# A gate projection: the input's forms at another byte, a second pass that takes two groups by sums, and a combination made in its result tiles

## The chip, the cores and the metric

The kernel runs on one core of one Trainium2 chip. The metric is the device time of one execution in microseconds (us). Three executions of the kernel before took 1046.55, 1047.09 and 1047.61 us: a median of 1047.09 us.

TensorE (PE) multiplies; VectorE (DVE), ScalarE (ACT) and GpSimd (POOL) do everything else; SyncE (SP) issues the loads of the weights. Each engine takes its instructions in the order in which the program lists them for it.

## The reference

One layer of a gated linear attention mixer and a squared-ReLU MLP, on 256 tokens of width 2048, all in float32. Cut to what matters:

```python
def layer(x):                                    # x: 256 x 2048
    h = rmsnorm(x, gla_norm)
    q, k, v, r, g_low = split(h @ w_in)          # w_in: 2048 x 6160; r: 256 x 2048
    log_a = log_sigmoid(g_low @ w_gate_up + b_gate) / 16
    o = chunked_gated_scan(q, k, v, log_a)       # 4 heads, chunks of 64 tokens
    o = o * rsqrt(mean(o * o) + eps) * o_norm    # per head of 512 columns
    x = x + (o * silu(r)) @ w_out
    a = relu(rmsnorm(x, mlp_norm) @ w_up)        # 256 x 8192
    x = x + (a * a) @ w_down
    return rmsnorm(x, final_norm)
```

The change concerns the product that gives `r`, and what is done with it.

## The kernel before, in words

**High and low parts.** TensorE multiplies in a float32 form of reduced precision. So each operand is kept as a high part (a copy in that form) and a low part (the value less its high part), and a product is three matmuls: high by high, high by low, low by high (`multiply`, L664 to L670; the matmul itself is L669). The weights arrive as plain float32. ScalarE makes the high part of each piece (L1201), VectorE the low part (L1207). A matmul here always has a stationary block of 128 x 128 and 256 moving columns.

**Gate projection.** `r` is made in four passes c = 0 to 3 of 512 columns. Each pass has four groups g of four K tiles of 128 rows, so a group's weights are 128 partitions x 2048 elements, 1 MB. A group of a pass is called a double, (c,g). It is done in one of two ways:
- plain (`plain_double`): the tokens are stationary, the weights move, 48 matmuls;
- by sums (`sums_double`): a 2 x 2 block scheme that needs seven products of blocks where the plain way needs eight. 24 matmuls read parts of the weights as they are, and 18 read sums of blocks of them, 42 in all. On the token side the scheme needs sums of the input too. These are the input's forms `x_forms` (L536), made once for g = 2 and 3, and kept in a tile named `h` in the trace.

What a sums double needs of the weights is made as follows. First the block add: a quarter of the weights is added to another, in place. In this projection VectorE does it (first line of `adds`, L859); in the later product with `w_out` ("o") GpSimd issues a DMA within SBUF that accumulates (`add_block`, L845). Then VectorE makes three sums of blocks (rest of `adds`), ScalarE their high part (L869 and L870), and VectorE their low part (L520). The sums have one buffer (`sums`), and so have their parts (`sumshl`), so that two sums doubles can't be prepared far apart from their use. The weights have three buffers (`rawu0` to `rawu2`) and three of high and low parts (`high`, `low`), taken in turn.

**Banks and the combination.** A pass by sums accumulates in four banks of PSUM: T0B, T1B, B16 and B50. A plain pass takes two, T0B and T1B. Banks come from one list: who needs a bank takes the first, who is done appends it. After a pass by sums, `combine_parts` (L945) puts the four banks together: ScalarE copies B16 to SBUF (L949), VectorE does six additions and subtractions (L519 and L520, four of 128 x 256 and two of 128 x 512). The scratch for that is `ends`, the first half of the tile `sums` (L581). Then each half goes through a silu on ScalarE (L982) and is multiplied into the attention's result `on` on VectorE (L986). After a plain pass `gated` (L921) does the silu out of the bank.

**Attention in between.** Between the parts of pass 0 stand the eight products of the attention ("attends", four heads of two token tiles). Each puts its result in a bank. ScalarE squares it and sums up (`attend_square`, L892), VectorE scales the sum (L898), GpSimd takes its power of -1/2 (`rsqrt`, L314) and multiplies it by a factor of the token (L902). Last ScalarE puts the scaled result into `on` (`attend_put`, L906), and only then is the bank free.

**The order.** The doubles before, in program order: pass 0 plain 0, sums 2, plain 1, sums 3, with an attend at each gap; pass 1 plain 0, 1, 2, 3; pass 2 plain 0, sums 2, eight transposes, plain 1, sums 3; pass 3 plain 0 to 3. A plan sets the order of all other work: `at(time, run)` enters it with a time counted in matmuls of TensorE's program, all entries are sorted by it, and each engine gets its instructions in that order. `chunk` enters the high and low parts and the load of a group (L842, on SyncE's queue). For a plain double of a later pass of the gate projection these stand 89, 70 and 173 ahead of its first matmul; for a sums double 80, 63 and 204, the three adds 94, the casts of the sums 50 and 41, the low part of the sums 30. `place_chunks` assigns the three places for parts in order of the high parts.

**The result of a pass.** `some512` gives a tile of 128 x 512, named `sr` in the trace, one for each half of the tokens.

Of the kernel before, what the change touches and what calls it, by code (L numbers as in the profile page):

```python
# [70 lines left out]
def tile_gla_mlp(ctx, tc, x, xt, w_vg, w_in, w_gate, w_out, w_up, w_down, final_norm, out):  # L71
# [460 lines left out]
    def sums_of_rows(a):  # L532
        return a.rearrange("p (n b f s) -> p n b f s", n=2, b=2, f=4)

    hbuf = h_tile(F32R)
    x_forms = {g: sums_of_rows(hbuf[:, OFF + n * 2 * G : OFF + (n + 1) * 2 * G]) for n, g in enumerate((2, 3))}  # L536
    on = None

    def take_on():
# [38 lines left out]
    slot += [a_slot(1), a_slot(2)]  # L578
    by_form = lambda a: a.rearrange("p (f b c) -> p f b c", f=3, b=2)
    sums = by_form(flat_sums)  # L580
    ends = flat_sums[:, : 3 * T].rearrange("p (f s) -> p f s", f=3)  # L581
    sums_to = o_stage = None

    def take_sums():
# [33 lines left out]
    def at(time, run):  # L618
        plan.append((time, len(plan), run))
# [151 lines left out]
    plain_double("r", 0, 1, between=one_attend)  # L771
    sums_double("r", 0, 3, between=one_attend)
    end_of("r", 0)
    for g in range(4):
        plain_double("r", 1, g)
    end_of("r", 1)
    plain_double("r", 2, 0)
    sums_double("r", 2, 2)
# [54 lines left out]
    for n, (p, c, g, summed_) in enumerate(doubles):  # L833
# [10 lines left out]
        def add_block(view=view):  # L844
            nc.gpsimd.dma_start(out=view[:, :, 1, left], in_=view[:, :, 1, right], accum_op=ALU.add)  # L845

        here = p == "r"
        if not summed_:
            early = 14 if here and c else 0
            chunk(key, time - UP_HI - early, time - UP_LO - early, time + 2 * UP, (time - UP_EARLY - 3 * early, load), raw)  # L850
            continue
        early = 13 if here and c else 0
        chunk(key, time - 67 - early, time - 50 - early, time + RAWS, (time - 165 - early, load), raw)
        if not here:
            at(time - 116, add_block)

        def adds(view=view, here=here):
            if here:
# [6 lines left out]
            sub(sums_to[1], sums, sums_to[0].bitcast(F32))  # L865
            done.add(("sums", key))

        at(time - 68 - 2 * early, adds)
        at(time - 50, lambda: nc.scalar.copy(sums_to[0][:, :2], sums[:, :2]))  # L869
        at(time - 41, lambda: nc.scalar.copy(sums_to[0][:, 2], sums[:, 2]))  # L870
        at(time - 30, low)
# [61 lines left out]

        return run, times

    for c in (1, 3):
        e = mark("end", "r", c)
        for t in range(NT):
            run, times = gated(c, t, None)
            at(e - 5 + 6 * t, run)  # L940
            at(e + 2 + 7 * t, times)

    pair = lambda a: a.rearrange("p (i s) -> p i s", i=2)

    def combine_parts(p, c, out0, out1):  # L945
        pc = p, c

        def first():
            nc.scalar.copy(ends[:, 1:3].rearrange("p f s -> p (f s)"), bank_of[pc, B16])  # L949
            release(pc, B16)  # L950

        def second():
            sub(ends[:, 2], ends[:, 1], ends[:, 2])
            sub(ends[:, 0], bank_of[pc, B50][:, left], ends[:, 2])
            add(pair(out0()), pair(bank_of[pc, T0B]), ends[:, 0:2])
            release(pc, T0B)

        def third():
            both = bank_of[pc, B50][:, right]
            add(ends[:, 0], both, ends[:, 0])  # L960
            sub(ends[:, 2], ends[:, 2], both)
            release(pc, B50)
            add(pair(out1()), pair(bank_of[pc, T1B]), ends[:, 0::2])
            release(pc, T1B)

        e = mark("end", p, c)
        for n, run in ((-11, first), (-6, second), (1, third)):
            at(e + n, run)
        return e

    for c in (0, 2):
        zs = {}

        def new(t, zs=zs):
            zs[t] = some512()
            return zs[t]

        e = combine_parts("r", c, lambda new=new: new(0), lambda new=new: new(1))
        for t in range(NT):

            def silu(t=t, zs=zs):
                nc.scalar.activation(zs[t], zs[t], AF.Silu, scale=r1[:, t : t + 1])  # L982

            def times(c=c, t=t, zs=zs):
                o = on[:, t, c * GT : (c + 1) * GT]
                nc.vector.tensor_tensor(o, o, zs[t], op=ALU.mult)  # L986

            at(e + 4 + 8 * t, silu)
            at(e + 11 + 8 * t, times)
# [618 lines left out]
```

## Time and profile before

| what | value |
|---|---|
| median of three executions | 1047.09 us (1046.55 to 1047.61) |
| profiled execution: its time | 1046.55 us |
| its span | 1044.7 us |
| mean granted clock of TensorE | 0.998 |
| busy: PE, DVE, ACT, POOL | 1036.4, 850.8, 689.7, 92.5 us |
| chain of waits: share of PE | 98% |
| DMA | 228.21 MB, mean 218 GB/s |

The trace is of one execution. Its time is 1.85 us more than its span, which begins at the first and ends at the last recorded instruction. Times in rows are microseconds from the span's start. A row of a timeline has the start, the duration, the engine, the line, the operation and tiles (written <- read), the shape, the types, how many equal ones follow each other, and, in square brackets, the idle time of the engine just before it with what ended it. A tile's number is left out there. A row of a table of windows has the window, its length, then for PE, weight load, DVE, ACT, POOL and SyncE the busy time and the count, then the granted clock, the busy share of the DMA engines, and GB/s. The gate projection runs from about 150 to 325 us.

### The profile page before, as it was taken

What the parts mean: (1) busy time and instruction counts of PE and PEld (TensorE: products, weight loads), DVE (VectorE), ACT (ScalarE), POOL (GpSimd) and SP (SyncE); (2) the same over time, 40 slices, a digit from 0 to 9 for tenths busy, and PEclk for the clock granted to TensorE, in tenths of its full rate; (3) what the DMA queues carried; (4) which work ended last, traced back from release to release, by engine and by line L of the source; (5) the groups of instructions that cost most, each with busy time, mean ns of one, the idle gap of its engine ahead of it and who ended that gap; (6) DMA issues with size and microseconds to landing.
All of it is one profiled execution on the core that took longest, in us unless ns stands there. A gap on an engine that the chain in (4) does not pass through costs nothing.

```text
span 1044.7 us, 21232 instructions
## 1 busy us (share of the span) xinstructions
PE 1036.4 (99%) x9050; PEld 1036.2 (99%) x9050; DVE 850.8 (81%) x856; ACT 689.7 (66%) x824; POOL 92.5 (9%) x105
## 2 busy tenths in 40 slices
PE   9999999999999999999999999999999999999997
PEld 9999999999999999999999999999999999999997
DVE  7568657667687776899989989989989999999894
ACT  7675545574575664667677677777767667768763
POOL 0000000120000001010101101011111101010000
PEclk9999999999999999999999999999999999999999
DMA  9857664454766576787878778787788788787652
GB/s 346 310 164 212 194 201 147 137 199 164 263 191 215 155 267 193 217 256 226 231 228 250 223 223 252 222 234 231 223 246 236 211 255 232 208 255 229 201 208 81
DMA packets 117438, 228.21 MB, mean 218 GB/s; under 512 B 6192, under 2 KB 22576, under 8 KB 117216
## 3 DMA queue, kind: packets, MB, share of 16 engines
q1 hardware_dynamic: 99920, 208.84, 60.5%
q0 software_dynamic: 16320, 15.73, 9.7%
q10 hardware_dynamic: 1104, 2.29, 0.6%
q8 instruction: 70, 1.15, 0.4%
q14 instruction: 24, 0.20, 0.0%
HBM read 209.02 MB, written 2.10 MB: 202 GB/s over the span
## 4 chain that ended last, share of the span: by engine, by line
PE 98%; issue 1%; ACT 0%; DVE 0%; POOLq 0%; POOL 0%; ACTq 0%
PE acc L1363 21%; PE acc L1243 18%; PE aux L1243 16%; PE acc L669 12%; PE acc L149 11%; PE acc L181 6%; PE aux L669 4%; PE aux L1363 4%; PE aux L181 2%; PE aux L149 2%; PE aux L216 0%; PE acc L739 0%; PE acc L479 0%; PE aux L479 0%; ACT sqf L1497 0%
## 5 line engine op out<-in xcount | busy, mean ns | idle before, releaser
L1207 DVE TENSOR_TENSOR low<-rawu,high 128x2048 fp32r<-128x2048 f32 (+1 forms) x101 | 224.6, 2226 | 26.3 <-ACT high L1201 24.3
L1201 ACT CAST high<-rawu 128x2048 fp32r<-128x2048 f32 (+1 forms) x101 | 187.4, 1857 | 47.2 <-DMA rawu<-in_w_up 12.6
L1243 PE MATMUL acc<-hh,high 128*128 128x256 f32 x544 | 150.6, 277 | 0.0
L1243 PE MATMUL acc<-hh,low 128*128 128x256 f32 x544 | 150.5, 277 | 0.0
L1243 PE MATMUL acc<-hl,high 128*128 128x256 f32 x544 | 150.5, 277 | 0.0
L1412 ACT CAST sumshl<-sums 128x1024 fp32r<-128x1024 f32 x112 | 88.2, 835 | 94.0 <-PE acc L1363 70.6
L1207 DVE TENSOR_TENSOR low<-rawd,high 128x2048 fp32r<-128x2048 f32 (+1 forms) x59 | 132.8, 2252 | 17.7 <-ACT high L1201 17.7
L1201 ACT CAST high<-rawd 128x2048 fp32r<-128x2048 f32 (+1 forms) x59 | 111.4, 1890 | 44.8 <-PE acc L1243 36.7
L520 DVE TENSOR_TENSOR sumshl<-sums,sumshl 128x1536 fp32r<-128x1536 f32 x64 | 112.3, 1755 | 25.2 <-ACT sumshl L1412 24.7
L1243 PE MATMUL aux<-hh,high 128*128 128x256 f32 x480 | 132.8, 277 | 0.0
L1243 PE MATMUL aux<-hl,high 128*128 128x256 f32 x480 | 132.8, 277 | 0.0
L1243 PE MATMUL aux<-hh,low 128*128 128x256 f32 x480 | 132.7, 277 | 0.0
L1363 PE MATMUL acc<-high,acts 128*128 128x256 f32 x598 | 116.0, 276 | 0.0
L119 DVE TENSOR_TENSOR lo<-raw,hi 128x1024 fp32r<-128x1024 f32 (+3 forms) x68 | 78.7, 1164 | 44.3 <-ACT hi L118 44.1
L1399 POOL DMA_DIRECT2D rawd<-rawd x56 | 67.6, 1207 | 515.4 <-DVE sums L519 264.5
L118 ACT CAST hi<-raw 128x1024 fp32r<-128x1024 f32 (+3 forms) x68 | 67.7, 1001 | 56.0 <-PE acc L181 25.7
L1243 PEld LDWEIGHTS acc<-hh,high 128*128 128x128 f32 x544 | 102.2, 188 | 0.0
L1243 PEld LDWEIGHTS acc<-hl,high 128*128 128x128 f32 x544 | 102.2, 188 | 0.0
L1243 PEld LDWEIGHTS acc<-hh,low 128*128 128x128 f32 x544 | 102.2, 188 | 0.0
L1363 PEld LDWEIGHTS acc<-high,acts 128*128 128x128 f32 x598 | 96.6, 188 | 0.0
L1363 PE MATMUL acc<-sumshl,acts 128*128 128x256 f32 x720 | 96.0, 276 | 0.0
L1243 PEld LDWEIGHTS aux<-hh,high 128*128 128x128 f32 x480 | 90.2, 188 | 0.0
(346 smaller groups left out, 2788.1 us busy)
## 6 DMA issues: line engine op xcount, KB each, us to landing
rawu<-in_w_up SPq DMA_DIRECT2D x124, 512.0 KB, 4.5
rawd<-in_w_down SPq DMA_DIRECT2D x56, 1024.0 KB, 5.1
raw<-in_w_in SPq DMA_DIRECT2D x48, 512.0 KB, 4.7
rawu<-in_w_in SPq DMA_DIRECT2D x16, 1024.0 KB, 5.0
rawu<-in_w_out SPq DMA_DIRECT2D x16, 1024.0 KB, 5.8
rawd<-rawd POOLq DMA_DIRECT2D x56, 256.0 KB, 5.3
rawu<-in_w_down SPq DMA_DIRECT2D x16, 512.0 KB, 4.4
raw<-in_w_vg SPq DMA_DIRECT2D x13, 520.0 KB, 8.4
```

Source lines behind the costliest of these rows:

```text
L118: last_hi[0] = nc.scalar.copy(hi[:, s], raw[:, s])
L119: last_lo[0] = nc.vector.tensor_tensor(lo[:, s], raw[:, s], hi[:, s].bitcast(F32), op=ALU.subtract)
L149: nc.tensor.matmul(o[:, m], x, w[:, m], start=first and c == 0, stop=last, skip_group_check=True)
L181: nc.tensor.matmul(o, u[:, s], m[:, kt], start=kt == 0 and n == 0 and j % 2 == 0, stop=kt == KT - 1 and n == 2, skip_group_check=True,)
L520: sub = lambda o, x, y: nc.vector.tensor_tensor(o, x, y, op=ALU.subtract)
L669: nc.tensor.matmul(b[:, o], a[x], w[y], start=(pc, name) in fresh, stop=last and i == 2, skip_group_check=True)
L1201: nc.scalar.copy(o, i)
L1207: nc.vector.tensor_tensor(o, i, x.bitcast(F32), op=ALU.subtract)
L1243: nc.tensor.matmul(o, w[:, s], row_h(kt)[m], start=kt == 0 and n == 0 and j % 2 == 0, stop=kt == KT - 1 and n == 2, skip_group_check=True,)
L1363: nc.tensor.matmul(bank[:, o], a[x], w[y], start=fresh and i == 0, stop=d + 1 in starts + [SUMMED] and i == 2, skip_group_check=True,)
L1399: nc.gpsimd.dma_start(out=view[:, :, 1, left], in_=view[:, :, 1, right], accum_op=ALU.add)
L1412: nc.scalar.copy(sums_to[0][:, f], sums[:, f])
```

## The change

Three things are edited.

1. The input's forms lie at the start of their tile, where they stood 48 elements (192 bytes) behind it. Counted in SBUF, their blocks then start at byte 192 modulo 256, where they started at byte 128.
2. Pass 1 is done as plain 0, sums 2, plain 1, sums 3, where it was plain 0 to 3. Its two block adds are done by the accumulating DMA on GpSimd's queue, not by VectorE; passes 0 and 2 keep VectorE's.
3. `combine_parts` has no scratch of its own: ScalarE copies the bank B16 in two halves into the two result tiles, and the four small and two large operations work in place there. It is used for passes 0, 1 and 2 of `r` and for passes 1 and 3 of `o`; pass 1's silu thus comes from the result tile and no longer from the bank.

```diff
     hbuf = h_tile(F32R)
-    x_forms = {g: sums_of_rows(hbuf[:, OFF + n * 2 * G : OFF + (n + 1) * 2 * G]) for n, g in enumerate((2, 3))}
+    x_forms = {g: sums_of_rows(hbuf[:, n * 2 * G : (n + 1) * 2 * G]) for n, g in enumerate((2, 3))}
...
-    ends = flat_sums[:, : 3 * T].rearrange("p (f s) -> p f s", f=3)
...
-    for g in range(4):
-        plain_double("r", 1, g)
+    plain_double("r", 1, 0)
+    sums_double("r", 1, 2)
+    plain_double("r", 1, 1)
+    sums_double("r", 1, 3)
     end_of("r", 1)
...
-        here = p == "r"
+        here = p == "r" and c != 1
         if not summed_:
-            early = 14 if here and c else 0
+            early = 14 if p == "r" and c else 0
...
-        early = 13 if here and c else 0
+        early = 13 if p == "r" and c else 0
         chunk(key, time - 67 - early, time - 50 - early, time + RAWS, (time - 165 - early, load), raw)
         if not here:
-            at(time - 116, add_block)
+            at(time - 116 - early, add_block)
...
-        at(time - 68 - 2 * early, adds)
+        at(time - 68 - (2 if here else 0) * early, adds)
...
-    for c in (1, 3):
+    for c in (3,):
...
-    pair = lambda a: a.rearrange("p (i s) -> p i s", i=2)
-
     def combine_parts(p, c, out0, out1):
         pc = p, c
+        z = []
 
         def first():
-            nc.scalar.copy(ends[:, 1:3].rearrange("p f s -> p (f s)"), bank_of[pc, B16])
+            z.extend((out0(), out1()))
+            for i, o in enumerate((left, right)):
+                nc.scalar.copy(z[i][:, right], bank_of[pc, B16][:, o])
             release(pc, B16)
 
         def second():
-            sub(ends[:, 2], ends[:, 1], ends[:, 2])
-            sub(ends[:, 0], bank_of[pc, B50][:, left], ends[:, 2])
-            add(pair(out0()), pair(bank_of[pc, T0B]), ends[:, 0:2])
-            release(pc, T0B)
+            sub(z[1][:, right], z[0][:, right], z[1][:, right])
+            sub(z[0][:, left], bank_of[pc, B50][:, left], z[1][:, right])
 
         def third():
             both = bank_of[pc, B50][:, right]
-            add(ends[:, 0], both, ends[:, 0])
-            sub(ends[:, 2], ends[:, 2], both)
+            add(z[1][:, left], both, z[0][:, left])
+            sub(z[1][:, right], z[1][:, right], both)
             release(pc, B50)
-            add(pair(out1()), pair(bank_of[pc, T1B]), ends[:, 0::2])
-            release(pc, T1B)
+            for i, name in enumerate((T0B, T1B)):
+                add(z[i], bank_of[pc, name], z[i])
+                release(pc, name)
...
-    for c in (0, 2):
+    for c in range(3):
```

From the second edit on, line numbers of the changed kernel are one lower (lines 581 to 772) to two higher than those of the kernel before.

The order of the instructions moves with it. In the rows below, numbers behind a name tell buffers of one name apart, and the square brackets name what is waited for: the other engines, DMAHW for loads, DMASW for DMAs of GpSimd's queue.

GpSimd, before, from the factor of the second head (`ors_2558`) to that of the fourth (`ors_2731`):

```order
L902 TENSOR_TENSOR ors_2558<-ors_2558,r1k_127 128x2 [waits Pool_49]
L314 TENSOR_TENSOR ors_2643<-oss_2583,mhalf_116 128x1 [waits DVE_49]
L314 TENSOR_TENSOR ors_2643<-oss_2583,mhalf_116 128x1 [waits Activation_49]
L902 TENSOR_TENSOR ors_2643<-ors_2643,r1k_127 128x2 [waits Pool_49]
L314 TENSOR_TENSOR ors_2731<-oss_2672,mhalf_116 128x1 [waits DVE_49,Activation_49]
L314 TENSOR_TENSOR ors_2731<-oss_2672,mhalf_116 128x1 [waits Activation_49]
```

And now; `rawu2` holds the weights of (1,2), `rawu1` those of (1,3):

```order
L903 TENSOR_TENSOR ors_2558<-ors_2558,r1k_127 128x2 [waits Pool_49]
L846 DMA rawu2_2348<-rawu2_2348 128x2x256 [waits DMAHW4_49,DMAHW5_49,DMAHW3_49,DMAHW6_49,DMAHW2_49,DMAHW7_49,DMAHW1_49,DMAHW0_49]
L314 TENSOR_TENSOR ors_2644<-oss_2583,mhalf_116 128x1 [waits DVE_49]
L314 TENSOR_TENSOR ors_2644<-oss_2583,mhalf_116 128x1 [waits Activation_49]
L903 TENSOR_TENSOR ors_2644<-ors_2644,r1k_127 128x2 [waits Pool_49]
L846 DMA rawu1_2347<-rawu1_2347 128x2x256 [waits DMAHW6_49,DMAHW1_49]
L314 TENSOR_TENSOR ors_2740<-oss_2674,mhalf_116 128x1 [waits DVE_49,Activation_49]
```

The two block adds stand between the factors of the heads, the first one behind that of the second head and the second one behind that of the third.

ScalarE around the same place, before: `rawu2` holds the weights of (1,1), `aux_1893` and `aux_1894` are the two banks of the third head's attends, `acc_1763` is pass 0's B16.

```order
L892 ACTIVATE sq_2640,oss_2583<-aux_1894,r1k_127 128x512 [waits PE_49,Activation_49]
L1201 CAST high2_2351<-rawu2_2348 128x2048 [waits DMAHW7_49]
L892 ACTIVATE sq_2673,oss_2672<-acc_1765,r1k_127 128x512 [waits PE_49,Activation_49]
L906 ACTIVATE on_1999<-aux_1893,ors_2643 128x512 [waits Pool_49]
L949 COPY sums_2345<-acc_1763 128x512 [waits DVE_49,PE_49]
L906 ACTIVATE on_1999<-aux_1894,ors_2643 128x512
L892 ACTIVATE sq_2708,oss_2672<-acc_1766,r1k_127 128x512 [waits PE_49,Activation_49]
L982 ACT_TABLE_LOAD
L982 ACTIVATE sr_2694<-sr_2694,r1_126 128x512 [waits DVE_49]
```

And now, with `rawu2` those of (1,2):

```order
L893 ACTIVATE sq_2641,oss_2583<-aux_1894,r1k_127 128x512 [waits PE_49,Activation_49]
L1202 CAST high2_2351<-rawu2_2348 128x2048 [waits DMAHW7_49,DMASW0_49]
L893 ACTIVATE sq_2675,oss_2674<-acc_1765,r1k_127 128x512 [waits PE_49,Activation_49]
L907 ACTIVATE on_1999<-aux_1893,ors_2644 128x512 [waits Pool_49]
L951 COPY sr_2694<-acc_1763 128x256 [waits PE_49,Activation_49]
L951 COPY sr_2695<-acc_1763 128x256 [waits Activation_49]
L907 ACTIVATE on_1999<-aux_1894,ors_2644 128x512
L870 CAST sumshl_2357<-sums_2345 128x1024 [waits DVE_49,PE_49]
L893 ACTIVATE sq_2714,oss_2674<-acc_1766,r1k_127 128x512 [waits PE_49,Activation_49]
L1202 CAST high0_2343<-rawu0_2346 128x2048 [waits DMAHW0_49]
L983 ACT_TABLE_LOAD [waits DVE_49]
L983 ACTIVATE sr_2694<-sr_2694,r1_126 128x512 [waits Activation_49]
```

The high part now also waits for the block add (DMASW), and behind it stands the put of `aux_1893`, the bank that the first matmul of (1,0) takes. A cast of sums and a high part stand ahead of the first silu that were not there before.

VectorE, before, from the low part of (1,0) (`low1_2350`) to the combination of pass 0 (`sr_2694` and `sr_2712` are its result tiles):

```order
L1207 TENSOR_TENSOR low1_2350<-rawu1_2347,high1_2349 128x2048 [waits DMAHW6_49,Activation_49]
L898 TENSOR_SCALAR oss_2583<-oss_2583 128x2 [waits Activation_49]
L1207 TENSOR_TENSOR low2_2352<-rawu2_2348,high2_2351 128x2048 [waits DMAHW7_49,PE_49,Activation_49]
L520 TENSOR_TENSOR sums_2345<-sums_2345 128x256 [waits Activation_49]
L520 TENSOR_TENSOR sums_2345<-acc_1764,sums_2345 128x256 [waits DVE_49,PE_49]
L519 TENSOR_TENSOR sr_2694<-acc_1895,sums_2345 128x512 [waits DVE_49]
```

And now:

```order
L1208 TENSOR_TENSOR low1_2350<-rawu1_2347,high1_2349 128x2048 [waits DMAHW6_49,Activation_49]
L899 TENSOR_SCALAR oss_2583<-oss_2583 128x2 [waits Activation_49]
L519 TENSOR_TENSOR sums_2345<-rawu2_2348 128x512 [waits DMAHW7_49,DMASW0_49,DVE_49]
L519 TENSOR_TENSOR sums_2345<-sums_2345,rawu2_2348 128x512 [waits DVE_49]
L520 TENSOR_TENSOR sums_2345<-sums_2345,rawu2_2348 128x512
L1208 TENSOR_TENSOR low2_2352<-rawu2_2348,high2_2351 128x2048 [waits PE_49,Activation_49]
L520 TENSOR_TENSOR sr_2695<-sr_2694,sr_2695 128x256 [waits Activation_49]
L520 TENSOR_TENSOR sr_2694<-acc_1764,sr_2695 128x256 [waits DVE_49,PE_49]
L519 TENSOR_TENSOR sr_2695<-acc_1764,sr_2694 128x256 [waits DVE_49]
L520 TENSOR_TENSOR sr_2695<-sr_2695,acc_1764 128x256
L519 TENSOR_TENSOR sr_2694<-acc_1895,sr_2694 128x512 [waits DVE_49]
```

Three adds stand between the scale of the third head and the low part, the first of them waiting for the block add; and both large operations of the combination now stand last.

## The prediction

> **What bounds the kernel now.** I read the page first, then TensorE's waits, then its pace stage by stage, and last VectorE's margins in the gate projection (pass c and group g of it: "(c,g)"; pass 1 is the "second gate pass").
>
> ```profile
> PE 1036.4 (99%) x9050; PEld 1036.2 (99%) x9050; DVE 850.8 (81%) x856; ACT 689.7 (66%) x824; POOL 92.5 (9%) x105
> PE aux L216 <- DVE square L213: 1.1, 1, 1.1
> 161.00:198.00 37.00, 37.00 (x329) 37.00 (x328) 25.23 (x30) 19.67 (x22) 0.00 (x0) 1.00 0.43 143
> 199.00:252.00 53.00, 53.00 (x452) 53.00 (x451) 38.55 (x40) 33.63 (x42) 10.36 (x12) 1.00 0.57 189
> 262.00:293.00 31.00, 31.00 (x266) 31.00 (x265) 20.52 (x22) 17.53 (x19) 0.00 (x0) 1.00 0.71 241
> L669 PE MATMUL acc<-high,h x24: 274/281/283, 198.5 to 263.1; 128*128 128x256 f32 x24
> ```
>
> TensorE never waits after its first microsecond, so time is matmuls times pace. The three stretches (length, then matmuls in brackets) give 37.00/329 = 112.5 ns, 53.00/452 = 117.3 and 31.00/266 = 116.5 ns at a full clock. The pace falls by about 4.4 ns as the first stationary block from `h` (the input's forms) comes at 198.5, and the matmuls on other operands between them are slow too.
>
> The second thing to see is how little VectorE is ahead here:
>
> ```profile
> 244.75 1.75 DVE L520 TENSOR_TENSOR sumshl<-sums,sumshl 128x1536 fp32r<-128x1536 f32 x1
> 250.90 0.88 PE L669 MATMUL acc<-sumshl,h 128*128 128x256 f32 x6
> 274.21 2.29 DVE L1207 TENSOR_TENSOR low<-rawu,high 128x2048 fp32r<-128x2048 f32 x1
> 276.73 0.28 PE L669 MATMUL acc<-low,xh 128*128 128x256 f32 x1
> 219.00:253.00 34.00, 34.00 (x291) 34.00 (x290) 26.55 (x28) 20.16 (x21) 1.26 (x3) 1.00 0.55 185
> ```
>
> The low part of (2,2)'s sums ends at 246.50 and is used at 250.90: 4.4 us early. The low part of (3,2) ends at 276.50 and is used at 276.73: 0.2 us early. Between these two ends VectorE's line takes 30.0 us, waits included. In 219 to 253 it is busy 26.55 of 34.00 us.
>
> **What the change gives.** Two plain doubles of 48 matmuls become sums doubles of 42: 12 x 0.1125 = 1.35 us. The forms move by 192 bytes to where the other stationary blocks lie. If that keeps the pace, some 735 matmuls between 198.5 and 293 (the 452 and 266 of the slow stretches, and their edges) gain 4.4 ns each, 3.25 us. With nothing late that is 4.6 us. The rows show the pace beside the tile, not its cause; for the 3.25 I take all, the other end is 0.
>
> The Trainium skill speaks against this term: "TensorE: Matmul & The Clock Gate", section "Back-to-back issue gap", gives a gap set by the number of columns alone, whatever the place of the operands. By it the two stretches would have one pace; the rows 4.4 ns apart at one clock disagree, and by it the sum would be 1.35 us instead of 4.6.
>
> **What it adds.** VectorE gets, in pass 1, twice three adds and a low part of sums, six operations of a combination, and no block add. The rows for these:
>
> ```profile
> 308.50 0.69 DVE L519 TENSOR_TENSOR sums<-rawu 128x512 f32<-128x512 f32 x1
> 310.49 2.29 DVE L1207 TENSOR_TENSOR low<-rawu,high 128x2048 fp32r<-128x2048 f32 x1
> 312.70 1.75 DVE L520 TENSOR_TENSOR sumshl<-sums,sumshl 128x1536 fp32r<-128x1536 f32 x1
> 314.37 2.29 DVE L1207 TENSOR_TENSOR low<-rawu,high 128x2048 fp32r<-128x2048 f32 x1
> ...
> 219.67 0.42 DVE L520 TENSOR_TENSOR sums<-sums 128x256 f32<-128x256 f32 x1
> 222.90 0.69 DVE L986 TENSOR_TENSOR on<-on,sr 128x512 f32<-128x512 f32 x1
> 223.51 0.16 DVE L898 TENSOR_SCALAR oss<-oss 128x2 f32<-128x2 f32 x1
> 235.78 0.68 DVE L519 TENSOR_TENSOR rawu<-rawu 128x512 f32<-128x512 f32 x1
> 237.84 0.68 DVE L520 TENSOR_TENSOR sums<-sums,rawu 128x512 f32<-128x512 f32 x1
> ```
>
> Start to start: three adds 1.99, a low part 2.21, a low part of sums 1.67, a combination 3.23, a product with `on` 0.61, four adds 2.7. Pass 1 adds 2 x 3.66 + 3.23 = 10.5 us: 26.55 + 10.5 = 37 us of VectorE in a stretch that TensorE would pass in 34.0 - 1.35 - 1.3 = 31.4. The 4.4 us of lead don't cover 5.7.
>
> Worse is where the block add of (1,2) goes. GpSimd's queue takes it behind the second head's factor; ScalarE's high part and VectorE's first add then wait for its landing, each with its queue behind it.
>
> ```profile
> 207.63 4.19 POOL L314 TENSOR_TENSOR ors<-oss,mhalf 128x1 f32<-128x1 f32 x2 [4.05 <-DVE oss L898]
> 211.90 1.78 POOL L902 TENSOR_TENSOR ors<-ors,r1k 128x2 f32<-128x2 f32 x1
> 213.65 0.37 SPq L842 DMA_DIRECT2D rawu<-in_w_in  x1
> 300.73 1.35 POOL L845 DMA_DIRECT2D rawu<-rawu  x1 [75.58 <-issue]
> 300.98 0.37 SPq L842 DMA_DIRECT2D rawu<-in_w_out  x1
> 312.81 0.37 SPq L842 DMA_DIRECT2D rawu<-in_w_out  x1
> 313.19 1.21 POOL L845 DMA_DIRECT2D rawu<-rawu  x1 [11.11 <-DVE low L1207]
> 320.41 0.69 DVE L519 TENSOR_TENSOR sums<-rawu 128x512 f32<-128x512 f32 x1 [3.76 <-issue]
> DMA to landing us min/median/max: 3.6/5.5/7.7
> ```
>
> The factor ends at 211.90 + 1.78 = 213.68; with TensorE 0.3 us earlier by then, the add is issued at 213.4. The four block adds of this form took 3.6 to 7.7 us to land (last row). The two with a weight load issued within 0.4 us (300.98 beside 300.73, 312.81 beside 313.19) are the long ones: the second held VectorE until 320.41, 7.2 us. SyncE's row at 213.65 is the load that will be (1,3)'s, as before (only (1,2)'s and (1,1)'s change places): it waits for the low part of (1,0), at whose end GpSimd's factor ends too, so it starts beside the new add. So I take 7.4, of the 3.6 to 7.7 that bound it: **landing at 220.8**, where VectorE's queue would reach the adds at about 216.
>
> ScalarE: behind the high part stand a square, then the put that frees the bank for (1,0)'s first matmul.
>
> ```profile
> 194.45 1.04 ACT L869 CAST sumshl<-sums 128x1024 fp32r<-128x1024 f32 x1
> 215.53 1.91 ACT L1201 CAST high<-rawu 128x2048 fp32r<-128x2048 f32 x1
> 217.32 0.70 ACT L892 ACTIVATE sq<-acc,r1k 128x512 f32<-128x512 f32 x1
> 217.99 0.70 ACT L906 ACTIVATE on<-aux,ors 128x512 f32<-128x512 f32 x1
> 219.03 0.73 ACT L906 ACTIVATE on<-aux,ors 128x512 f32<-128x512 f32 x1
> 219.79 0.28 PE L669 MATMUL aux<-high,xh 128*128 128x256 f32 x1
> 220.85 1.28 ACT L982 ACT_TABLE_LOAD   x1
> ```
>
> From 215.53 to the end of the put, 218.69, is 3.2 us; so (1,0) starts at 220.8 + 3.2 = 224.0, where it stood at 219.79: 4.2 us late at once. (Pass 1 now takes four banks for two; the third and fourth are first written by (1,2), 5.4 us after (1,0)'s start, and free by then: the combination of pass 0 reads the last of them at about 227.) The high part, square, put, copy and second put (to 219.76, 4.2 us), a cast of sums (0.95), a square (0.67), a high part (1.8), the table load (1.28, no longer ahead of the wait) and a silu (0.7) put the first silu's end 9.6 us behind the landing; VectorE, with three adds, a low part and a combination (7.4), waits 2.2 us for it.
>
> VectorE from the landing to the end of (2,2)'s low part of sums: five low parts 11.05, three low parts of sums 5.0, adds 6.7, two combinations 6.45, three products 1.85, a copy 0.35: 31.4 us, and waits for ScalarE of 2.2, 0.3 and 0 to 1 (0.5): 34.4 us. That is 255.2 against 246.50. TensorE alone, from 224.0 over 252 matmuls, would be there at 252.4: VectorE binds. From there the 30.0 us of line to (3,2) are unchanged in work (its first silu comes 1.2 us later, since both adds stand last; the shorter copies give part of it back), while TensorE, from 250.90 to 276.73, needs 25.8, and 25 at the better pace. (3,2) starts at 285.3 for 276.73: 8.5 us late. The rest of the stage, some 147 matmuls, gains 0.65 back. Nothing later changes but the copy of the combination, 0.5 us on ScalarE, under matmuls at a margin of 3 us.
>
> Sum: 1046.55 (the profiled execution) + 8.5 - 0.65 = 1054.4; it lay 0.54 below the median, so **1054.9**.
>
> **Rivals.**
> 1. The add lands alone, 3.6 to 3.9 us after 213.4, because the load of (1,3) is served behind it. For it: the two short adds; against it: the loads 0.25 and 0.38 us from the long ones. All of the sum is 3.7 us earlier: 1051.2.
> 2. The wait cools TensorE. The last matmuls and the clock after them (the eighth figure of the windows):
>
> ```profile
> 1036.64 0.84 PE L149 MATMUL acc<-hl,acts 128*128 128x256 f32 x6
> 1040.00:1044.70 4.70, 0.00 (x0) 0.00 (x0) 0.00 (x0) 0.02 (x1) 0.00 (x0) 0.53 0.58 225
> 1.06 4.63 PE aux L216 x20
> ```
>
> The clock is near half from about 3 us after the last matmul; at the start 4.6 us passed before full pace. The wait at (1,0), about 5 us, is that long; those from (3,0) to (3,2) come to 5 us in pieces. At (1,0) the loss vanishes under VectorE, which is 2.8 us later than TensorE at (2,2); at (3,2) half a rate over 4.6 us costs up to 2.3: 1057.2. The Trainium skill has this as a rule ("TensorE: Matmul & The Clock Gate", section "Part 1: The HAM clock gate"): a free-running window of about 3.4 us without work drops the clock to half. By that rule a wait of 4 or 5 us may or may not hold a whole window.
> 3. Faster: VectorE keeps up. The 30.0 us of its line hold 6.8 us of waits (row below); if they vanish as TensorE comes earlier, and the add has landed by 213, when VectorE reaches it, nothing is late and all 4.6 us stay: 1042.5.
>
> ```profile
> 246.50:276.50 30.00, 23.19 (x28) 1.00 0.59 198
> ```
>
> For it: some of these waits are for TensorE, and come earlier with it. Against it: GpSimd is held to 213.7 by its factor. The point from which it decides: with the waits as they are, a landing at 213.0, 7.8 us before mine, gives the time of before. With half of this, an early landing and half the waits gone, the time is about 1047.
> 4. The place of the forms does nothing to the pace: the sum loses only the last 0.65, as VectorE binds anyway: 1055.5.
>
> **How the numbers follow.** Forecast 0.55, with its own range 1052.8 to 1056.8 (landing 219 to 222, the waits 0 to 1); rival 1 0.18; rival 2 0.10; rival 4 0.05; rival 3 0.05, its half 0.07. The range 1049.3 to 1057.5 leaves out rival 3 with its half and the far ends of 1 and 2. A measurement of this kernel tells about 0.2%, 2.1 us, from no change: faster 0.05 (rival 3), same 0.08 (its half, and the near edge of rival 1), slower 0.87.
>
> **What would show it.** Right: a wait of TensorE of 3 to 6 us ahead of (1,0), put down to ScalarE; some 5 us in all ahead of (3,0) to (3,2) for VectorE, most at (3,2); a block add from about 213.5 that lands near 220.8; a pace of 112.5 ns from 199 to 252 outside the waits; 9038 matmuls. Wrong: no idle time of TensorE in 219 to 286, or a landing before 214; then the sum of VectorE's line is what failed. A pace of 117 ns there takes the 3.25 away.

## The result, and the profile after

Five executions of the changed kernel took 1055.97 to 1059.32 us, with a median of 1057.6 us; the kernel before took 1047.09 us beside them. The ratio is 1.0095 (95% interval 1.0080 to 1.0109): slower by about 10 us. The forecast was 1054.9 us. The median lies outside the forecast's own range (1052.8 to 1056.8 us) and 0.1 us above the wider one, which ended at 1057.5 us; by the ratio the time is 1.0095 x 1047.09 = 1057.0 us.

The profiled execution was the slowest of the five: 1059.32 us, a span of 1057.5 us, a mean granted clock of 0.992. That is 12.8 us more than the profiled execution before. The other four had clocks of 0.993 to 0.996, and their times fall as the clock rises: 1058.29 us at 0.993, 1057.60 at 0.994, 1056.04 and 1055.97 at 0.996.

TensorE's waits in the kernel after (engine, tile and line, what it waited for; total, times, longest). Before, there were none behind the first microsecond:

```profile
PE aux L668 <- ACT on L907: 4.9, 1, 4.9
PE aux L668 <- DVE low L1208: 3.3, 2, 2.9
PE acc L668 <- DVE sumshl L520: 1.1, 1, 1.1
PE acc L668 <- DVE otl L752: 0.2, 1, 0.2
```

They come to 9.5 us. The timeline of the kernel after has them in order, and what they waited for:

```profile
213.75 1.34 POOL L846 DMA_DIRECT2D rawu<-rawu  x1
213.79 0.37 SPq L843 DMA_DIRECT2D rawu<-in_w_in  x1
220.96 1.90 ACT L1202 CAST high<-rawu 128x2048 fp32r<-128x2048 f32 x1 [5.18 <-DMA rawu<-rawu]
221.02 0.69 DVE L519 TENSOR_TENSOR sums<-rawu 128x512 f32<-128x512 f32 x1 [5.04 <-DMA rawu<-rawu]
223.44 0.68 ACT L907 ACTIVATE on<-aux,ors 128x512 f32<-128x512 f32 x1
224.17 0.58 PE L668 MATMUL aux<-high,xh 128*128 128x256 f32 x1 [4.95 <-ACT on L907]
...
255.33 1.75 DVE L520 TENSOR_TENSOR sumshl<-sums,sumshl 128x1536 fp32r<-128x1536 f32 x1
257.14 0.74 PE L668 MATMUL acc<-sumshl,h 128*128 128x256 f32 x4 [1.09 <-DVE sumshl L520]
...
284.67 2.28 DVE L1208 TENSOR_TENSOR low<-rawu,high 128x2048 fp32r<-128x2048 f32 x1
287.00 0.58 PE L668 MATMUL aux<-low,xh 128*128 128x256 f32 x1 [2.88 <-DVE low L1208]
```

The first six rows are the chain that the prediction described. The block add and the load are issued 0.04 us apart. Both users of the added weights start at 221, 7.2 us behind the issue. ScalarE's put ends at 224.12, and (1,0) starts at 224.17. The other two pairs are (2,2) and (3,2). (3,2) starts its low part at 287.00, where the kernel before had 276.73.

Waits are not all. The table of windows shows what TensorE did between them (window, length, PE, weight load, DVE, ACT, POOL, clock, DMA share, GB/s):

```profile
199.00:219.00 20.00, 20.00 (x179) 20.00 (x177) 11.60 (x12) 10.70 (x18) 10.41 (x10) 1.00 0.66 210
224.00:228.00 4.00, 3.83 (x18) 3.83 (x19) 3.86 (x7) 4.00 (x8) 0.00 (x0) 0.50 0.37 95
228.20:255.60 27.40, 27.40 (x234) 27.40 (x234) 22.15 (x25) 15.48 (x19) 4.28 (x3) 1.00 0.52 171
265.00:271.80 6.80, 6.80 (x63) 6.80 (x61) 5.00 (x5) 2.35 (x6) 0.00 (x0) 1.00 0.47 154
287.00:293.00 6.00, 6.00 (x28) 6.00 (x29) 4.69 (x3) 2.14 (x3) 0.00 (x0) 0.50 0.81 281
293.40:306.60 13.20, 13.20 (x115) 13.20 (x114) 5.37 (x4) 5.09 (x4) 0.00 (x0) 1.00 0.34 121
```

Three paces can be seen. Up to the first wait, 20.00/179 = 111.7 ns: the forms' new place does keep the pace. Right behind two of the waits, about 213 ns: the granted clock is 0.50 in 224 to 228 and in 287 to 293. And then, at a full clock, 27.40/234 = 117.1 and 13.20/115 = 114.8 ns, with the blocks in the same place as in 199 to 219. Between (265 to 271.8, behind the transposes) the good pace is back: 6.80/63 = 107.9 ns by the counts, 113.3 ns by the distances of the starts (a window also counts the two or three matmuls that it cuts, which matters in a short one).

So a ledger of the stage can be made, by the distances between the starts of matmuls from about 160.5 us to the 24 matmuls behind the second set of transposes. The stretch took 137.8 us before and 150.7 us now. (All stretches of this kind are good to 0.2 us, since some matmul records are missing.) 1172 recorded matmuls at an unbroken 113 ns and the transposes would take 133.0 us (a kernel below that never waits takes 134.4 us for 1184), so 17.7 us were lost:

| where | us |
|---|---|
| waits, with the slow first matmul behind each | 10.9 |
| half clock: 48 matmuls at 213 ns instead of 113 | 4.8 |
| slower pace: 434 matmuls at 117.7 ns instead of 113 | 2.0 |

The stage as a whole begins up to 0.6 us earlier or later than in the kernel before, so times from the span's start can be compared to about that; the stretch is free of it.

### The profile page after: what moved, and what is told of

It is laid out like the page before. It is cut to its first block, busy times and chain, and to the rows that moved or that the text cites. A ratio compares the mean times of both kernels' runs of the same rounds, so it can differ in the third digit from the quotient of the medians.

```text
span 1057.5 us, 21235 instructions
## 1 busy us (share of the span) xinstructions
PE 1039.9 (98%) x9038; PEld 1038.7 (98%) x9038; DVE 859.5 (81%) x870; ACT 693.8 (66%) x834; POOL 97.9 (9%) x107
## 4 chain that ended last, share of the span: by engine, by line
PE 72%; DVE 3%; ACT 1%; issue 1%; POOLq 0%; POOL 0%; ACTq 0%; DVEq 0%
PE acc L1244 32%; PE acc L1364 17%; PE aux L1364 8%; PE acc L668 7%; PE aux L668 2%; PE acc L149 2%; DVE low L1208 1%; PE aux L1244 1%; PE aux L149 1%; ACT high L1202 1%; DVE sumshl L520 0%; PE acc L738 0%; DVE sr L520 0%; DVE otl L752 0%; DVE sr L519 0%
## 5 line engine op out<-in xcount | busy, mean ns | idle before, releaser
L1244 PE MATMUL acc<-hh,high 128*128 128x256 f32 x992 | 274.1, 276 | 0.0
L1244 PE MATMUL acc<-hh,low 128*128 128x256 f32 x992 | 274.0, 276 | 0.0
L1244 PE MATMUL acc<-hl,high 128*128 128x256 f32 x992 | 274.0, 276 | 0.0
L1244 PEld LDWEIGHTS acc<-hh,high 128*128 128x128 f32 x992 | 186.3, 188 | 0.0
L1244 PEld LDWEIGHTS acc<-hh,low 128*128 128x128 f32 x992 | 186.3, 188 | 0.0
L1244 PEld LDWEIGHTS acc<-hl,high 128*128 128x128 f32 x992 | 186.3, 188 | 0.0
L1364 PEld LDWEIGHTS acc<-sumshl,acts 128*128 128x128 f32 x621 | 76.4, 188 | 0.0
L1364 PE MATMUL acc<-low,acts 128*128 128x256 f32 x230 | 63.5, 276 | 0.0
L1364 PE MATMUL aux<-high,acts 128*128 128x256 f32 x276 | 60.4, 276 | 0.0
L181 PE MATMUL acc<-xh,hi 128*128 128x256 f32 x192 | 53.0, 276 | 0.0
```

What stands on the lines that cost most here:

```text
L181: nc.tensor.matmul(o, u[:, s], m[:, kt], start=kt == 0 and n == 0 and j % 2 == 0, stop=kt == KT - 1 and n == 2, skip_group_check=True,)
L1244: nc.tensor.matmul(o, w[:, s], row_h(kt)[m], start=kt == 0 and n == 0 and j % 2 == 0, stop=kt == KT - 1 and n == 2, skip_group_check=True,)
L1364: nc.tensor.matmul(bank[:, o], a[x], w[y], start=fresh and i == 0, stop=d + 1 in starts + [SUMMED] and i == 2, skip_group_check=True,)
```

## The experiments

"Stretch" is the stretch of the ledger. Each kernel was timed beside the kernel before, whose median was 1046.54 to 1047.32 us in these sessions; the ratio is to that. The stretch and the waits are those of the one profiled execution.

| kernel | median us | ratio to before (95%) | stretch us | TensorE's waits in it, us |
|---|---|---|---|---|
| before | 1047.09 | | 137.8 | 0 |
| changed | 1057.60 | 1.0095 (1.0080 to 1.0109) | 150.7 | 9.5 |
| forms' place alone | 1044.23 | 0.9981 (0.9972 to 0.9990) | 135.6 | 0.3 |
| combination alone | 1047.13 | 1.0005 (0.9996 to 1.0014) | 138.4 | 0.4 |
| changed, early block add | 1052.49 | 1.0051 (1.0036 to 1.0067) | 144.2 | 5.6 |
| changed, VectorE's block adds | 1055.03 | 1.0075 (1.0062 to 1.0089) | 146.1 | 7.4 |
| changed, put first | 1056.49 | 1.0098 (1.0071 to 1.0126) | 146.7 | 9.2 |
| changed, forms' old place | 1058.24 | 1.0107 (1.0091 to 1.0122) | 150.7 | 8.8 |
| changed, no low sums | 1053.02 | 1.0053 (1.0040 to 1.0067) | 144.7 | 7.3 |
| changed, early add, no low sums | 1049.39 | 1.0020 (1.0011 to 1.0029) | 140.9 | 3.4 |
| forms' place, swapped product | 1045.02 | 0.9978 (0.9963 to 0.9993) | 134.4 | 0 |
| the same, a wait of 2.5 us put in | 1049.19 | 1.0026 (1.0016 to 1.0035) | 140.0 | 2.5 |
| the same, a wait of 6.1 us put in | 1053.51 | 1.0063 (1.0046 to 1.0080) | 144.6 | 6.1 |

### The forms' place alone

```diff
-    x_forms = {g: sums_of_rows(hbuf[:, OFF + n * 2 * G : OFF + (n + 1) * 2 * G]) for n, g in enumerate((2, 3))}
+    x_forms = {g: sums_of_rows(hbuf[:, n * 2 * G : (n + 1) * 2 * G]) for n, g in enumerate((2, 3))}
```

> The kernel before with the forms' place alone changed. Theory: the place of the stationary blocks sets TensorE's pace as long as nothing waits. Then the pace stays at 113.3 ns from 198.5 to 252 (117.9 before), and TensorE comes to (3,2) about 2.5 us earlier than 276.7, where VectorE's low part was only 0.2 us ahead; part of VectorE's 6.8 us of waits in its last 30 us shrinks with it. So a wait of 0 to 2.3 us there, and 1043.3 to 1046.0 us in all, 1044.5 as the value. Rival: the place does nothing, the pace falls at the first forms as before, 1046.5 us.

Measured: 1044.23 us. The waits of this kernel and two of its windows:

```profile
PE acc L669 <- DVE low L1207: 0.3, 1, 0.3
```

```profile
199.00:250.00 51.00, 51.00 (x452) 51.00 (x452) 38.12 (x39) 33.47 (x40) 10.35 (x12) 1.00 0.59 196
274.00:290.00 16.00, 15.95 (x135) 15.95 (x136) 9.26 (x7) 8.00 (x7) 0.00 (x0) 1.00 0.61 213
```

452 matmuls now take 51.0 us where they took 53.0: the place of the stationary blocks did set the pace. The wait at (3,2) is there too, 0.3 us long. Behind it the pace is 117.9 ns by the median distance, though nothing has changed its place. That was not expected, and the later experiments follow it up.

### The combination alone

The kernel before with the new `combine_parts`, used for the same passes as before.

> The kernel before with the combination in the result tiles alone. Theory: it lies under matmuls, no change, 1046.5 us. Rival: both large additions now stand last, so the first silu after a pass by sums comes 1.2 us later; the 0.2 us of lead at (3,2) is gone and TensorE waits about 1 us there: 1047.5 us and a slower pace behind it, up to 0.7 us more.

Measured: no difference in time (0.9996 to 1.0014). In the trace the lead at (3,2) is gone, as the rival said, though only half as far:

```profile
PE acc L669 <- DVE low L1207: 0.4, 1, 0.4
```

The stretch is longer by 0.6 us, under what the times can tell. So this edit hides almost everywhere, and costs about half a microsecond at the one place where VectorE has no lead.

### The block add of (1,2) issued early

```diff
-            at(time - 116 - early, add_block)
+            at(time - 116 - early - (35 if (p, c, g) == ("r", 1, 2) else 0), add_block)
```

> The changed kernel with the block add of (1,2) ahead of the second head's factor on GpSimd's queue: its weights landed at 206.7, so it can be issued there and lands by 210.3 to 214. Theory (two causes: the late landing and VectorE's line): the wait of 4.95 us at (1,0) goes, VectorE begins the adds at about 216.0 for 221.0, 5.0 us earlier, but its line still binds at (2,2) and (3,2): waits of 3 to 5 us there and 1050 us, up to 2.3 us more if the clock falls. Rival 1 (the landing was all): no wait left, 1042.5 to 1044. Rival 2 (VectorE's line was all): as the changed kernel, 1057 us.

Measured: 1052.49 us. GpSimd and VectorE in this kernel's timeline, and TensorE's waits:

```profile
207.41 1.35 POOL L846 DMA_DIRECT2D rawu<-rawu  x1 [3.56 <-DMA rawu<-in_w_in]
216.05 0.69 DVE L519 TENSOR_TENSOR sums<-rawu 128x512 f32<-128x512 f32 x1
```

```profile
PE aux L668 <- DVE low L1208: 3.4, 2, 2.9
PE acc L668 <- DVE sumshl L520: 1.8, 1, 1.8
PE aux L668 <- DVE sumshl L520: 0.4, 1, 0.4
```

The add is issued at 207.41, 2.7 us ahead of the next weight load, and lands 3.8 us later by the trace's DMA records, where beside a load it took 7.2. VectorE starts its adds at 216.05 with no wait for it, 5.0 us earlier, as expected. The wait at (1,0) is gone, the waits for VectorE are larger than they were (5.6 us, where 3 to 5 were expected), and (3,2) starts at 281.9 for 287.0, 5.1 us earlier. The clock fell twice, for 3.4 us each. The time is 0.2 us above what was allowed for that (1050 and 2.3). So there were two causes: neither "the landing was all" (1042.5 to 1044) nor "VectorE's line was all" (1057) fits.

### The block adds on VectorE

```diff
-        here = p == "r" and c != 1
+        here = p == "r"
```

> The changed kernel with the two block adds of the second gate pass on VectorE again. Theory: VectorE is 5.8 us earlier than in the changed kernel (it needn't wait for the landing at 221.0 and pays 0.7 twice), and its line still binds at (2,2) and (3,2): 1049.1 us, up to 2.3 us more if the clock falls. Rival (VectorE's line has no room for 1.4 us more, and the DMA was no cause): 1058 to 1059 us.

Measured: 1055.03 us, 3.6 us above the upper end of what was expected (1049.1 and 2.3) and 2.6 us faster than the changed kernel. (3,2) starts at 283.1, 3.9 us earlier than in the changed kernel and not 5.8. What I had left out: with `here` the adds are also entered 26 matmuls earlier, and the scale of the third head then stands behind the four adds on VectorE. So GpSimd's factor and ScalarE's put come later, TensorE waits 1.5 us at (1,0), and VectorE itself waits 3.1 us for the first silu. So by the medians and the stretch (146.1 for 150.7 us) the DMA of (1,2) was the worse choice at this place, but VectorE had no room for the adds either.

### The put ahead of the high part

```diff
+        late = 28 if (p, c, g) == ("r", 1, 2) else 0
-        chunk(key, time - 67 - early, time - 50 - early, time + RAWS, (time - 165 - early, load), raw)
+        chunk(key, time - 67 - early + late, time - 50 - early + late // 2, time + RAWS, (time - 165 - early, load), raw)
```

> The changed kernel with the high part of (1,2) behind the third head's two puts and the copies of pass 0's combination on ScalarE's queue (and VectorE's low part behind two small operations). Theory: the wait of 4.95 us at (1,0) shrinks to under 1 us, but the landing at 221 and VectorE's line behind it are as they were, so the same time is waited at (1,2) to (3,2) in other places: 1055 to 1058 us, depending on how often the clock falls. Rival (ScalarE's queue is what cost): no wait and no half clock at (1,0) and nothing late behind it, 1057.6 - 4.95 - 2.0 = 1050.6 us.

Measured: 1056.49 us. TensorE's rows with a wait from 217 to 234 in this kernel:

```profile
225.53 0.39 PE L668 MATMUL aux<-low,xh 128*128 128x256 f32 x1 [1.33 <-DVE low L1209]
231.35 0.84 PE L668 MATMUL aux<-sumshl,h 128*128 128x256 f32 x5 [2.72 <-DVE sumshl L520]
```

(1,0) starts without a wait, and (1,2) now waits 1.33 and 2.72 us for VectorE. All waits together are 9.2 us, for 9.5. So the wait that stood first in the list was worth little by itself: VectorE's line behind the landing held most of the same time. It held 1.1 us less, since VectorE waits 1.53 us for the first silu, for 2.63. The profiled execution, the fastest of four, gained more: its stretch is 4.0 us shorter, and its clock fell once, for 3.4 us, where the changed kernel's fell twice for 6.8. The medians are 1.1 us apart, with intervals that overlap.

### The forms' old place in the changed kernel

```diff
-    x_forms = {g: sums_of_rows(hbuf[:, n * 2 * G : (n + 1) * 2 * G]) for n, g in enumerate((2, 3))}
+    x_forms = {g: sums_of_rows(hbuf[:, OFF + n * 2 * G : OFF + (n + 1) * 2 * G]) for n, g in enumerate((2, 3))}
```

> The changed kernel with the input's forms at their old place. Theory: in the changed kernel the better pace lasted only from 198.6 to the wait at 219 and over some 70 matmuls in front of (3,0); what it gave there, about 0.8 and 0.2 us, ends in waits for the landing at 221 and for VectorE at (3,2). So no change: 1057.6 us within 1 us, the wait at (1,0) 0.8 us shorter. Rival (the place is worth here what it was alone): 1060 us.

Measured: 1058.24 us, and its first wait:

```profile
PE aux L668 <- ACT on L907: 4.1, 1, 4.1
```

0.8 us shorter than 4.9, with the same stretch of 150.7 us. An edit that saves 2.2 us of stretch alone (137.8 to 135.6) saves nothing here.

### Less of VectorE's line

Left out: the low parts of the sums of (1,2) and (1,3).

```diff
         def low(key=key):
-            sub(sums_to[1], sums, sums_to[0].bitcast(F32))
+            if key[1:3] != ("r", 1):
+                sub(sums_to[1], sums, sums_to[0].bitcast(F32))
```

> The changed kernel without VectorE's low parts of the sums of (1,2) and (1,3): 2 x 1.67 us of VectorE's line left out (the matmuls read what the buffer held). Theory: the landing and the wait at (1,0) stay, VectorE is 3.3 us earlier at (2,2) and (3,2), where TensorE waited 1.1 and 2.9 us: waits of 0 and about 1 us there, and 1053 to 1055.5 us, the lower if the clock doesn't fall at (3,2). Rival (the late landing is all, VectorE's line has room): no change, 1057.6 us.

Measured: 1053.02 us, with these waits:

```profile
PE aux L668 <- ACT on L908: 5.0, 1, 5.0
PE aux L668 <- DVE low L1209: 2.3, 1, 2.3
```

The wait at (1,0) stays, that at (2,2) is gone, and that at (3,2) is shorter by 0.6 us; the clock stays whole behind it.

With the early block add as well (both diffs above):

> Both at once: the early block add of (1,2), and no low parts of the sums of the second gate pass (left out). Theory: VectorE's low part of (3,2) ended at 281.8 with the early add; 3.3 us less of line puts it at 278.5, where the kernel before used it at 276.7: 1046.5 to 1049 us. Rival (another cause is left, such as the DMAs in SBUF slowing other work): above 1050 us.

Measured: 1049.39 us, 0.4 above the upper end. The waits:

```profile
PE aux L668 <- DVE low L1209: 3.4, 2, 2.9
```

(3,2) starts at 278.4, where 278.5 was expected. What lies above is a half clock behind that wait: 17 matmuls at 208 ns, 1.6 us. Early landing and a shorter line together take back about 8 of the changed kernel's 10.5 us; the rest is still VectorE at (3,2). Part of that isn't VectorE's own work: in this kernel as in the changed one, VectorE waits there for the second silu, which stands behind a high part on ScalarE.

```profile
284.06 0.69 DVE L987 TENSOR_TENSOR on<-on,sr 128x512 f32<-128x512 f32 x1 [1.73 <-ACT sr L983]
```

(This row is the changed kernel's. The kernel before waits 1.10 us at this place. Whether the edit of the next section would take the wait at (3,2) out of the changed kernel was not tried.)

### The swapped product: does a wait cost more than its length?

The forms' place alone, and VectorE's second product of pass 2 behind the low part of (3,2):

```diff
-            at(e + 11 + 8 * t, times)
+            at(e + 11 + 8 * t + (16 if (c, t) == (2, 1) else 0), times)
```

> The kernel before with the forms' new place, and one more edit: VectorE's second product with `on` of the third gate pass one place later, behind the low part of (3,2) that TensorE waited 0.3 us for. Theory (any wait, however short, turns TensorE's pace from 113.3 to 117.9 ns until the next transposes): the wait goes and with it the slow pace over 144 matmuls, 0.3 + 0.65 = 0.95 us: 1043.3 us. Rival (a wait costs its length): 0.3 us, 1043.9 us, and the pace behind 273.5 falls all the same.

Measured: no wait of TensorE in the stage, and this window:

```profile
262.00:290.00 28.00, 28.00 (x249) 28.00 (x248) 19.21 (x20) 16.19 (x16) 0.00 (x0) 1.00 0.76 254
```

28.00/249 = 112.4 ns all the way, where the kernel with the 0.3 us of wait had 118. The stretch is 134.4 us for 135.6: 1.2 us saved by taking away a wait of 0.3 us. The theory said 0.95, the rival 0.3. The times show neither: 1043.3 and 1043.9 us were expected, 1045.02 was measured, and the two kernels can't be told apart (1044.23 and 1045.02 us, intervals that overlap). Both are faster than the kernel before.

### One wait, put in

In the kernel just described, ScalarE does the third head's first put five times (or ten times) instead of once:

```diff
-        nc.scalar.activation(on[:, t, hd * DV : (hd + 1) * DV], o, AF.Copy, scale=rs[:, t : t + 1])
+        for _ in range(5 if (hd, t) == (2, 0) else 1):
+            nc.scalar.activation(on[:, t, hd * DV : (hd + 1) * DV], o, AF.Copy, scale=rs[:, t : t + 1])
```

> The kernel with the forms' new place and the swapped product, in which TensorE never waits, and one wait put into it: ScalarE does the third head's first put five times instead of once, so that (1,0) begins about 2.2 us late. Theory (a wait costs more than its length): 2.2 us, and the pace at 117.9 for 113.3 ns over some 280 matmuls until the next transposes, 1.3 us; and about 2 us more if the clock falls. The stretch of TensorE from 160.7 to 295.1, 134.4 us long there, becomes 137.9 or 139.9 us. Rival (a wait costs its length): 136.6 us and a pace of 113.3 behind it.

Measured: a wait of 2.5 us, a stretch of 140.0 us, 1049.19 us. Windows before, in and behind the wait:

```profile
199.00:218.00 19.00, 19.00 (x170) 19.00 (x170) 11.99 (x12) 13.38 (x20) 9.10 (x9) 1.00 0.65 215
218.20:221.00 2.80, 0.27 (x3) 0.07 (x1) 0.95 (x1) 2.70 (x5) 0.00 (x0) 1.00 0.26 34
221.00:222.30 1.30, 1.28 (x10) 1.28 (x11) 0.72 (x2) 1.30 (x3) 0.00 (x0) 1.00 0.97 345
222.30:225.80 3.50, 3.50 (x19) 3.50 (x18) 3.04 (x7) 3.47 (x5) 0.12 (x1) 0.51 0.40 151
226.00:255.00 29.00, 29.00 (x249) 29.00 (x248) 21.25 (x19) 15.04 (x14) 0.94 (x3) 1.00 0.50 167
```

111.8 ns before the wait, and 116.5 behind it until the transposes. The clock fell to half, but not in the wait: 1.3 us behind its end, and for 3.4 us. The stretch grew by 5.6 us: 2.7 for the wait, 1.6 for the half clock, 1.2 for the pace.

> The same with the put done ten times, so that (1,0) begins about 5.0 us late. Theory: 5.0 us, 1.3 us of slower pace, and a half clock for about 4 us behind the wait, 2.0 us: the stretch of 134.4 us becomes 142.7 us. Rival (a wait costs its length): 139.4 us, a full clock and a pace of 113.3 behind it.

Measured: a wait of 6.1 us (longer than meant), a stretch of 144.6 us, 1053.51 us. Behind the wait:

```profile
225.00:231.00 6.00, 6.00 (x29) 6.00 (x30) 3.76 (x8) 5.97 (x9) 1.26 (x3) 0.52 0.01 4
231.20:260.00 28.80, 28.80 (x247) 28.80 (x246) 21.15 (x19) 13.75 (x12) 0.00 (x0) 1.00 0.52 169
```

The stretch grew by 10.2 us: 6.3 for the wait, 2.9 for the half clock, 1.1 for the pace. (142.7 us were expected for a wait of 5.0 us.) A wait that costs its length is ruled out by both traces.

## Why the prediction was right, and where it was short

The mechanism came as described; the time was 2.7 us short in the median. That the wider range reached so far was owed to rival 2, the clock, and not to the forecast's own terms.

**What the change gives.** Right. Twelve matmuls and the pace were put at 4.6 us; 137.8 us before, and 133.0 us for the changed kernel's matmuls at an unbroken pace, are 4.8 us. That the place of the forms sets the pace is shown by the kernel that moves them alone; what it is about the place was not tried. But the prediction let the gain live through the waits, and it doesn't. The Trainium skill ("TensorE: Matmul & The Clock Gate", section "Back-to-back issue gap") gives the gap by the number of columns. This trace doesn't agree: the same 452 matmuls took 53.0 and 51.0 us at one clock.

**The late block add.** Right in every step: issue at 213.75 (213.4 said), beside the load, landing by 220.96 (220.8), (1,0) at 224.17 (224.0). That the load makes it long is shown: ahead of the load it took 3.8 us. All 13 traces say the same of the adds of this form in this stage and the product with `w_out`: 23 with a weight load issued within 0.6 us landed after 6.6 to 7.8 us; of 25 with none within 2.2 us, 24 took 3.6 to 4.4 us. Rival 1, the add alone, fell.

**VectorE binds.** Right. The early add removes the first wait and leaves the waits for VectorE; the put ahead of the high part only moves the wait; 3.3 us less of VectorE's line takes away the wait at (2,2) and part of that at (3,2). The waits are smaller than said: by the prediction VectorE is 2.8 us behind TensorE at (2,2) and some 5 us are waited from (3,0) to (3,2); 1.1 and 3.5 us were measured, since half a clock and the slower pace made TensorE late too. Rival 3 fell with that, and rival 4 by the first experiment.

**The size of VectorE's line.** Short by 1.9 us. The low part of (2,2)'s sums was to end at 255.2 and ended at 257.08. The term that failed is "waits for ScalarE of 2.2, 0.3 and 0 to 1 (0.5)", 3.0 us. In the trace they are 2.63 for the first silu, 1.26 for a high part, 0.97 for the cast of (1,3)'s sums and 0.26 for a silu: 5.1 us.

```profile
230.72 0.69 DVE L987 TENSOR_TENSOR on<-on,sr 128x512 f32<-128x512 f32 x1 [2.63 <-ACT sr L983]
239.14 2.29 DVE L1208 TENSOR_TENSOR low<-rawu,high 128x2048 fp32r<-128x2048 f32 x1 [1.26 <-ACT high L1202]
242.41 1.76 DVE L520 TENSOR_TENSOR sumshl<-sums,sumshl 128x1536 fp32r<-128x1536 f32 x1 [0.97 <-ACT sumshl L871]
254.72 0.69 DVE L987 TENSOR_TENSOR on<-on,sr 128x512 f32<-128x512 f32 x1 [0.26 <-ACT sr L983]
```

From there to the end at (3,2) 30.0 us were said and 29.9 measured.

**The clock.** This was rival 2 (0.10), put at 1057.2 us; it came true together with the forecast's mechanism. The clock fell at (1,0) and at (3,2) in the profiled execution. At (1,0) its 1.9 us vanished behind VectorE, as the rival had it. At (3,2) it cost 2.8 us, for "up to 2.3". I had treated it as something that needs a wait of 3 us or more, from the one place in the trace of before that shows it, the end. The runs show it behind waits of 1.8 us (in the kernel with the early add, at (2,2)) and 2.5 us, and not behind one of 2.9 us at (3,2) in the kernel with the put first. The Trainium skill ("TensorE: Matmul & The Clock Gate", section "Part 1: The HAM clock gate") asks for a free-running window of about 3.4 us that is idle. That the same wait may or may not bring it fits a window that runs freely; that 1.8 us were enough does not fit one that must be idle throughout. The five times that fall as the clock rises fit the first part.

The clock records of the traces say more. In each trace the granted clock changes only at points a whole number of 3.41 us apart (in the changed kernel 221.39, 228.21, 286.24 and 293.07); where they fall differs from trace to trace. Divide the stage at these points, and take the pieces that found the clock whole. All ten that held 2.08 us or more of TensorE's idle time ended in a half clock, none that held 1.71 us or less, and two of the five from 1.78 to 1.89 us. So it is not the length of a wait that decides, but how much of it falls into one piece: the 2.9 us at (3,2) with the put first were split into 1.88 and 0.99 us.

**The pace behind a wait.** Missing from the prediction. The last term, 0.65 us "gains back", was none. Of the waits in these traces 16 met the pace of 113 ns, and all 16 left it at 117.9 (some behind a half clock), the shortest with a matmul 0.16 us late. It then mostly stays there until the next transposes. But two waits that met the slow pace brought 113 ns back, for 16 and 7 matmuls, up to the next wait or half clock: the one at 231.35 with the put first, and the one at 278.37 with the early add and no low sums. So a wait can turn the pace both ways; what decides is open.

With the terms as measured the profiled execution comes out. (3,2) is 287.00 - 276.73 = 10.3 us late (8.5 said), the half clock behind it adds 2.8, and nothing is gained back: 13.1 us, and its time was 12.8 us longer. Half of the miss from 7.85 us is VectorE's waits for ScalarE with the gain that wasn't taken, the other half the clock. The median execution, 10.5 us slower, had less of half clock (a mean clock of 0.994 for 0.992).

## What to carry to other kernels

Where an engine never waits, what a change saves on it can be added up closely (4.6 us here, for 4.8); what decides is the lead of the engines that feed it. Write down each feeder's lead at its tightest use, and all that the change puts into its line up to there, its own waits for third engines included. When a wait turns up, ask what stands behind it in line before you remove it: taking away the longest wait gave about 1 us by the medians here, for 4.9, because the next ones held most of the same time. And look for the edit that needs no slack: of three, the 192 bytes alone were the gain.

## What the runs showed of the hardware

- A wait of TensorE costs more than its length. Here a wait that met the pace of 113.3 ns turned it to 117.9, even a wait of 0.3 us; where nothing came between, this lasted until the next set of transposes and the 24 matmuls behind it, over 144 matmuls (0.65 us) behind the wait of 0.3 us and some 250 (1.2 us) behind the one of 2.5. The same happens without a wait when a stationary block comes from another place (byte 128 modulo 256 here, where the others lie at 192; other places were not tried). Why the transposes mend it was not tried.
- The granted clock changes at points 3.41 us apart, and is halved where some 1.8 to 2.1 us or more of one such piece were idle. A wait of 1.8 us was enough, one of 2.9 us across two pieces was not. The half clock lasted one or two pieces, 3.41 or 6.83 us, with 15 to 29 matmuls at 213 ns in them: 1.5 to 2.9 us each time. It can begin 1.3 us after the wait has ended.
- A block add of 256 KB by DMA within SBUF landed in 3.8 us when the next weight load of 1 MB came 2.7 us later, and in 7.2 us beside one issued within 0.04 us; that load took 5.9 us for 5.0.
